# The second feed-forward product of a hybrid RWKV-7 / gMLP step, with seven block products in place of eight

## The chip, the cores and the metric

One core of one Trainium2 chip. The metric is the device time of one execution in microseconds (us); the time before is the median of three runs.

## The reference

One denoising step of a two-layer backbone. Two streams are taken together: 128 context tokens and 512 latent tokens, T = 640 columns of 1024 features. Each layer has an RWKV-7 branch and a chunked gMLP branch, a mix of both, and then the feed-forward part that the change touches:

```python
h2 = rmsnorm(x, p['norm2_g'][l]) * (1 + sc2) + sh2
x = x + g2 * (jnp.square(jax.nn.relu(h2 @ p['w1'][l])) @ p['w2'][l])
```

`w1` is 1024 x 4096, `w2` is 4096 x 1024, all in float32. Six modulation vectors (shift, scale and gate, twice) come from `silu(cond) @ w_ada + b_ada` for each layer and each of the two streams; `g2` is one of them. After the last layer follows one more RMSNorm with `final_g`.

## The kernel before, in words

Features lie on the 128 partitions, the 640 tokens along the free axis as two halves of HT = 320. A matrix of weights comes as blocks of 128x512 (four 128x128 weights side by side). `load_w` (L97 to L104) loads such a block, copies it on ACT to `hi` (the reduced type that TensorE takes, fp32r) and subtracts on DVE to get `lo`, the rest. Every product is three matmuls: `hi` by high part, `hi` by low part, `lo` by high part of the activations (`mm_block`, L106 to L113). `hi` and `lo` have four buffers each, the raw block three. `dense` (L115) makes one output block of 128 x 640 in a PSUM tile `dps` with a bank for each half; there are two such tiles, and four single banks in another pool (`psr`, tags `g` and `pu`). `dense_pair` (L262 on) makes two output blocks half by half, the first half of both before the second, so that what follows for the first half can start early; its weights are loaded and split once for each half.

The feed-forward part (mark `ff`) works in two halves of the hidden dimension. In each, 16 output blocks of the first product go through relu and square on ACT and are split into `fh` and `fl`; then the second product adds into `x`, with the hidden blocks as its inner dimension, block by block of the eight output blocks (`residual`, L271 to L276: one operation on DVE for each token range with its own gate, so 128, 192 and 320 columns). In the second half the last two output blocks go by `dense_pair`, and after each half of the tokens `after` adds to the sum of squares (`sumsq`) and starts the norm: that of layer 1 (`rms.norm`), or the final one (`fin`, L1018, with a store for each of the eight blocks).

In layer 0's first half the modulation of layer 1 is made as well. `mod_col` (L163) loads 128 columns of `w_ada` as 128x1024 and reduces it on DVE twice (once for each stream) against `silu(cond)`; 48 such columns, three after each hidden block.

All is unrolled. The framework orders each engine's instructions when the program is built: an instruction that stands earlier in the program goes first where its inputs and buffers are ready by its plan, and it sets all waits. On the chip each engine then takes its instructions in that fixed order. Loads go through SP's queue.

Of the kernel before, what the change touches and what calls it, by code (L numbers as in the profile page):

```python
# [33 lines left out]
GORD = (((0, 4), (4, 4), (8, 2)), ((0, 4), (8, 2), (4, 4)))  # L34
SP = {'n': (3, 2, 1, 2, 2, 1, 0, 0, 3, 1), 'v': 1, 'k': 4, 'r': 7, 'kk': 7, 'F': 200, 'B': None, 't': 10, 'g0': 2, 'gn': (2, 2, 2, 1, 2, 2, 2, 1)}
# [6 lines left out]
def emit(tc, I, O, depth=DEPTH, mark=lambda s: None):  # L42
    nc = tc.nc
    ctx = ExitStack()
    with ctx:
# [117 lines left out]
        def mod_col(l, j, scr):  # L163
# [95 lines left out]
        def wsrc(w):  # L259
            return lambda kb: w[:, kb * 512:(kb + 1) * 512]  # L260
# [46 lines left out]
        for l in range(depth):  # L307
# [73 lines left out]
            with tc.tile_pool(name=f"com{l}", bufs=1) as com:  # L381
# [543 lines left out]
                with tc.tile_pool(name=f"x{l}", bufs=1) as xpool:  # L925
# [38 lines left out]
                    with tc.tile_pool(name=f"ff{l}", bufs=1) as ff:  # L964
                        if l + 1 < depth:
                            mod_setup(l + 1)
                            silu_c(ff)
                        for half in range(2):
                            fh = ff.tile([128, 16, T], F32R, tag="fh", name="fh")
                            fl_ = ff.tile([128, 16, T], F32R, tag="fl", name="fl")  # L970
                            for m in range(16):
                                if half == 0 and m < 2:
                                    if m == 0:
                                        pss = dense_pair(wsrc(I["w1"][l, 0]), wsrc(I["w1"][l, 1]), hh, hl)
                                    ps = pss[m]
                                else:
                                    ps = dense(I["w1"][l, half * 16 + m], hh, hl)
                                t = ff.tile([128, T], F32, tag="nt", name="relu", bufs=3)
                                nc.scalar.activation(pv(t), ps[:, :, 0:HT], AF.Relu)
                                nc.scalar.activation(t, t, AF.Square)  # L980
                                split(fh[:, m], fl_[:, m], t)
                                if l + 1 < depth and half == 0:
# [95 lines left out]
```

## Time and profile before

| | |
|---|---|
| median of 3 runs | 3319.86 us (3317.98 to 3334.59) |
| the profiled execution | 3320.89 us, its span 3319.2 us |
| PE busy | 3129.1 us (94%), 26160 matmuls |
| DVE, ACT, POOL busy | 2156.9 (65%), 1509.4 (45%), 613.5 us (18%) |
| layer 0's feed-forward part | some 1222 to 1692 us |
| layer 1's feed-forward part | some 2847 to 3305 us |
| DMA queue q1 | 368.49 MB, 34.7% of 16 engines |

PE is the TensorE's matmuls, DVE VectorE, ACT ScalarE, POOL GpSimd. Of a matmul's busy time a good part overlaps the next one's, so the pace of matmuls is read from counts in a stretch and not from the length of one. "L111" is the line in the kernel. A group's name reads output<-inputs by the program's tile names. What stands after "<-" in brackets is what ended an idle time.

### The profile page before, as it was taken

Reading aid. Unit: us, or ns where it says so; the run is one execution under the profiler, and the core shown is the slowest. Engines: PE = TensorE matmul, PEld = TensorE weight load, DVE = VectorE, ACT = ScalarE, POOL = GpSimd, SP = SyncE. Lnnn points to the kernel's source line nnn. Section 1 sums busy time; section 2 is a strip of 40 time slices with the busy share of each in tenths; the row PEclk is TensorE's granted clock in tenths of the full one; section 3 lists DMA queues with packets and bytes.
Section 4 is the critical chain, followed back from the end, with each engine's and each line's share of the span. In section 5 each row is a group of like instructions: output and inputs, shape, how many; then the busy total and the mean of one; then the engine's idle time right before and its main releaser. Section 6 shows DMA issues by size and latency. Waiting matters only on the chain.

```text
span 3319.2 us, 66348 instructions
## 1 busy us (share of the span) xinstructions
PE 3129.1 (94%) x26160; PEld 2840.5 (86%) x26160; DVE 2156.9 (65%) x4147; ACT 1509.4 (45%) x3268; POOL 613.5 (18%) x616
## 2 busy tenths in 40 slices
PE   8999799999999999999999979999999999999998
PEld 7988677777778989999999967787777799899998
DVE  6777778878875468943363387788897735532334
ACT  5444444554555345224264434455554533541432
POOL 3004333333331010000010143333333200100000
PEclk7998889999999999999999989899999999999999
DMA  6683122222224626632344521122222345222223
GB/s 206 203 299 124 57 74 67 76 67 74 67 80 125 216 83 212 217 115 77 93 146 145 189 79 57 58 81 72 78 75 73 104 142 169 89 77 74 77 74 102
DMA packets 215671, 372.73 MB, mean 112 GB/s; under 512 B 63680, under 2 KB 72000, under 8 KB 215360
## 3 DMA queue, kind: packets, MB, share of 16 engines
q1 hardware_dynamic: 215360, 368.49, 34.7%
q8 instruction: 206, 3.38, 0.4%
q14 instruction: 105, 0.86, 0.1%
HBM read 288.41 MB, written 63.31 MB: 106 GB/s over the span
## 4 chain that ended last, share of the span: by engine, by line
PE 66%; DVE 18%; issue 5%; DMA 4%; ACT 4%; POOL 2%; SPq 0%; DVEq 0%; POOLq 0%; ACTq 0%
PE dps L111 43%; PE g L644 4%; DMA wada<-in_wada 3%; PE dps L491 3%; PE dps L256 3%; DVE D L676 2%; DVE X L678 2%; DVE wjunk L168 2%; PE pu L776 2%; PE pu L789 2%; PE pu L751 1%; PE pu L757 1%; PE pu L795 1%; DVE lo L103 1%; DVE XN L694 1%
## 5 line engine op out<-in xcount | busy, mean ns | idle before, releaser
L101 ACT ACTIVATE hi<-raw 128x512 fp32r<-128x512 f32 x630 | 396.2, 631 | 1006.6 <-PE dps L111 803.0
L103 DVE TENSOR_TENSOR lo<-raw,hi 128x512 fp32r<-128x512 f32 x550 | 393.9, 718 | 522.5 <-ACT hi L101 510.8
L111 PE MATMUL dps<-ah,hi 128*128 128x320 f32 x2768 | 685.2, 324 | 7.6 <-ACT up L468 4.1
L111 PE MATMUL dps<-ah,lo 128*128 128x320 f32 x2768 | 677.7, 321 | 0.0
L111 PE MATMUL dps<-al,hi 128*128 128x320 f32 x2768 | 677.6, 322 | 0.0
L111 PEld LDWEIGHTS dps<-ah,hi 128*128 128x128 f32 x2768 | 474.5, 192 | 26.7 <-ACT up L468 5.2
L111 PEld LDWEIGHTS dps<-ah,lo 128*128 128x128 f32 x2768 | 474.2, 192 | 14.5 <-issue 0.4
L111 PEld LDWEIGHTS dps<-al,hi 128*128 128x128 f32 x2768 | 475.0, 192 | 13.2 <-issue 0.4
L168 DVE CUSTOM_DVE_ANT_0 wjunk<-wada,sc 128x1024 f32<-128x1024 f32 x176 | 221.9, 1261 | 34.2 <-DMA wada<-in_wada 32.2
L785 POOL TENSOR_TENSOR sw<-SV,wc 64x128 f32<-64x128 f32 x288 | 150.6, 523 | 450.5 <-DVE SV L803 438.6
L644 PE MATMUL g<-LA,BK 64*128 64x128 f32 x1280 | 183.1, 315 | 34.2 <-POOL BK L625 13.4
L103 POOL TENSOR_TENSOR lo<-raw,hi 128x512 fp32r<-128x512 f32 x80 | 118.2, 1477 | 511.8 <-ACT hi L101 425.5
L111 PE MATMUL dps<-fh,lo 128*128 128x320 f32 x896 | 204.6, 310 | 3.4 <-DVE lo L103 3.4
L644 PEld LDWEIGHTS g<-LA,BK 64*128 64x128 f32 x1280 | 153.4, 211 | 62.2 <-issue 23.6
L111 PE MATMUL dps<-fh,hi 128*128 128x320 f32 x896 | 204.3, 309 | 0.0
L111 PE MATMUL dps<-fl,hi 128*128 128x320 f32 x896 | 204.1, 309 | 0.0
L676 DVE TENSOR_TENSOR D<-AA,X 128x30 f32<-128x30 f32 (+14 forms) x480 | 182.6, 380 | 24.3 <-POOL X L671 14.2
L678 DVE TENSOR_TENSOR X<-X,D 128x30 f32<-128x30 f32 (+14 forms) x480 | 176.3, 367 | 10.5
L249 POOL TENSOR_TENSOR al<-nt,ah 128x320 fp32r<-128x320 f32 x24 | 26.7, 1114 | 705.1 <-ACT ah L248 704.0
L625 POOL TENSOR_TENSOR BK<-ta,cum 64x640 f32<-64x640 f32 x64 | 128.3, 2004 | 139.2 <-DVE ta L616 108.3
L111 PEld LDWEIGHTS dps<-fh,lo 128*128 128x128 f32 x896 | 149.6, 188 | 4.7 <-DVE lo L103 4.7
L111 PEld LDWEIGHTS dps<-fl,hi 128*128 128x128 f32 x896 | 149.9, 188 | 0.0
(293 smaller groups left out, 5773.8 us busy)
## 6 DMA issues: line engine op xcount, KB each, us to landing
raw<-in_w SPq DMA_DIRECT2D x280, 256.0 KB, 2.6
raw<-in_win SPq DMA_DIRECT2D x234, 256.0 KB, 2.8
wada<-in_wada SPq DMA_DIRECT2D x88, 512.0 KB, 4.1
ld<-up SPq DMA_DIRECT2D x80, 320.0 KB, 3.5
th<-ld SPq DMA_DIRECT2D x32, 320.0 KB, 3.0
ta<-ld SPq DMA_DIRECT2D x32, 320.0 KB, 3.1
gd<-spill SPq DMA_DIRECT2D x32, 320.0 KB, 2.3
raw<-in_wo SPq DMA_DIRECT2D x40, 256.0 KB, 2.6
```

Source lines behind the costliest of these rows:

```text
L101: nc.scalar.activation(hi, raw, AF.Copy)
L103: (eng or nc.vector).tensor_tensor(lo, raw, hi.bitcast(F32), ALU.subtract)
L111: nc.tensor.matmul(ps[:, n, 0:HT], w[:, k * 128:(k + 1) * 128], xk[:, n * HT:(n + 1) * HT], start=(first and k == 0 and j == 0), stop=(las ...
L168: nc.vector.tensor_tensor_reduce(junk, wt, sc_cur[0][:, v, :], 1.0, 0.0, ALU.mult, ALU.add, mods[l][:, j, v:v + 1])
L256: nc.tensor.matmul(ps[:, n, 0:HT], w[:, k * 128:(k + 1) * 128], x[:, 4 * kb + k, hs(n)], start=(kb == 0 and k == 0 and j == 0), stop=(kb = ...
L491: nc.tensor.matmul(o, x[:, k, tk * 128:(tk + 1) * 128], w[:, kk * 256:(kk + 1) * 256], start=(k == 0 and j == 0 and tk % 2 == 0), stop=(k ...
L625: nc.gpsimd.tensor_tensor(b[s, c, 1 - h, :], rt[s], e[s], ALU.mult)
L644: nc.tensor.matmul(gs[h][:, c - c0, :], b[s, c, :, :].rearrange("p x t -> p (x t)"), la[s, c, h:h + 2, :].rearrange("p x t -> p (x t)"), s ...
L676: nc.vector.tensor_tensor(t3, AA[:, s + 1:32, s:s + 1].to_broadcast([128, n, s]), X[:, s:s + 1, 0:s].to_broadcast([128, n, s]), ALU.mult)
L678: nc.vector.tensor_tensor(X[:, s + 1:32, 0:s], X[:, s + 1:32, 0:s], t3, ALU.add)
L776: nc.tensor.matmul(pu[64 * h:64 * h + 64, d, 0, :], LA[d][:, cs[d], 2 * h, :], SV[:, us[d], h, :], start=(d == 0), stop=True, skip_group_c ...
L785: nc.gpsimd.tensor_tensor(sw[s], SV[s, both, h, :], wcu[s, both].unsqueeze(2).to_broadcast([64, 2, L]), ALU.mult)
```

## The change

The second product works in quarters of the hidden dimension (1024, that is eight hidden blocks) and in pairs of output blocks. For a pair and a quarter the weights are four blocks A11, A12 (first output block, inner blocks 0 to 3 and 4 to 7) and A21, A22 (second), 512 deep and 128 wide; the hidden activations are four blocks B11, B12 (inner blocks 0 to 3, first and second half of the tokens) and B21, B22. Eight products of such blocks become seven (Strassen's scheme in Winograd's form), each of four 128-deep steps with three matmuls of 128x320:

- `hidden` makes relu and square of eight hidden blocks, then T1 to T4 by subtraction (on POOL, for the last j on DVE), and splits all seven activation blocks into `FH`, `FL`. In layer 0 both `lo` of each `w1` block are made on POOL, in layer 1 one of the two.
- `combine` loads the four weight blocks and makes S1 to S4 by four operations on POOL, one pair ahead of use.
- `strassen` splits A11, A12, A22 and S1 to S4 (some on POOL), accumulates in four PSUM tiles a, b, c, d, copies a on ACT and adds on DVE (`u2`, `u3`, `s1`), and adds the four results into `x`. In the first pair of a quarter (`lead`) the first three products go first in their three leading steps.
- Layer 1's modulation is made by `mod_halves` in 96 steps with 512-wide reductions, four after each hidden block with j < 3 and two after each pair, in quarters 0 to 2; the remaining sums are added at its end.
- After the last pair's first half `done` starts the norm of the first half, as before; the final norm's multiplications and stores for both halves come after the second.

The diff, cut (the lines taken out are those of the kernel above; indentation shortened):

```diff
--- before
+++ after
+WB, HB = 4, 1
...
+        def mod_halves(l, scr):
+            macc = scr.tile([128, 48, 2], F32, tag="macc", name="macc")
+            for hf in range(2):
+                w = slice(512 * hf, 512 * hf + 512)
+                sc = scr.tile([128, 2, 512], F32, tag="sch", name="sch")
+                for v in range(2):
+                    nc.sync.dma_start(sc[:, v, :], I["cc"][v:v + 1, w].to_broadcast([128, 512]))
+                    th = scr.tile([128, 512], F32, tag="wjh", name="silu")
+                    nc.scalar.activation(th, sc[:, v, :], AF.Tanh, scale=0.5)
+                    nc.vector.scalar_tensor_tensor(th, th, 1.0, sc[:, v, :], ALU.add, ALU.mult)
+                    nc.vector.tensor_scalar(sc[:, v, :], th, 0.5, None, ALU.mult)
+                for j in range(48):
+                    wt = scr.tile([128, 512], F32, tag="wah", name="wah", bufs=3)
+                    nc.sync.dma_start(wt, I["wada"][l, j, :, w])
+                    junk = scr.tile([128, 512], F32, tag="wjh", name="wjh")
+                    for v in range(2):
+                        acc = macc[:, j, v:v + 1] if hf else mods[l][:, j, v:v + 1]
+                        nc.vector.tensor_tensor_reduce(junk, wt, sc[:, v, :], 1.0, 0.0, ALU.mult, ALU.add, acc)
+                    yield
+            nc.vector.tensor_tensor(mods[l], mods[l], macc, ALU.add)
...
-with tc.tile_pool(name=f"ff{l}", bufs=1) as ff:
+with tc.tile_pool(name=f"ff{l}", bufs=1) as ff, ExitStack() as ctx_l:
     if l + 1 < depth:
         mod_setup(l + 1)
-        silu_c(ff)
...
+    B11, B21, B22, T1, T2, T3, T4, B12 = range(8)
+    def w1src(m):
+        return wsrc(I["w1"][l, m])
+    def w2raw(m, q, kb):
+        return I["w2"][l, m, q, :, kb * 512:(kb + 1) * 512]
+    def hidden(q):
+        FH = ff.tile([128, 7, 4, HT], F32R, tag="fh", name="fh")
+        FL = ff.tile([128, 7, 4, HT], F32R, tag="fl", name="fl")
+        for j in range(4):
+            H = ff.tile([128, 8, HT], F32, tag="H", name="H", bufs=HB)
+            ms = (8 * q + j, 8 * q + j + 4)
+            if q == 0 and j == 0:
+                pss = dense_pair(w1src(ms[0]), w1src(ms[1]), hh, hl)
+            for z, m in enumerate(ms):
+                ps = pss[z] if q == 0 and j == 0 else dense(I["w1"][l, m], hh, hl, engs=(nc.gpsimd if l + 1 < depth else None, nc.gpsimd))
+                o = H[:, B11:B12 + 1:7, :] if z == 0 else H[:, B21:B22 + 1, :]
+                nc.scalar.activation(o, ps[:, :, 0:HT], AF.Relu)
+                nc.scalar.activation(o, o, AF.Square)
+                mod_some(4 if j < 3 else 0)
+            split(FH[:, 0:3, j, :], FL[:, 0:3, j, :], H[:, 0:3, :])
+            e = nc.vector if j == 3 else nc.gpsimd
+            e.tensor_tensor(H[:, T1], H[:, B12], H[:, B11], ALU.subtract)
+            e.tensor_tensor(H[:, T3], H[:, B22], H[:, B12], ALU.subtract)
+            e.tensor_tensor(H[:, T2], H[:, B22], H[:, T1], ALU.subtract)
+            e.tensor_tensor(H[:, T4], H[:, B21], H[:, T2], ALU.subtract)
+            split(FH[:, 3:7, j, :], FL[:, 3:7, j, :], H[:, 3:7, :])
+        return FH, FL
+    def combine(q, m0, m1):
+        A = {}
+        for z, m in enumerate((m0, m1)):
+            for kb in range(2):
+                t = A[z, kb] = ff.tile([128, 512], F32, tag="ar", name="ar", bufs=6)
+                nc.sync.dma_start(t, w2raw(m, q, kb))
+        S = [ff.tile([128, 512], F32, tag="sr", name="sr", bufs=4) for _ in range(3)]
+        nc.gpsimd.tensor_tensor(S[0], A[1, 0], A[1, 1], ALU.add)
+        nc.gpsimd.tensor_tensor(S[1], S[0], A[0, 0], ALU.subtract)
+        nc.gpsimd.tensor_tensor(A[1, 0], A[0, 0], A[1, 0], ALU.subtract)
+        nc.gpsimd.tensor_tensor(S[2], A[0, 1], S[1], ALU.subtract)
+        S.insert(2, A[1, 0])
+        return A[0, 0], A[0, 1], A[1, 1], S
+    def strassen(m0, m1, W, FH, FL, half, lead):
+        A11, A12, A22, (S1, S2, S3, S4) = W
+        a = psr.tile([128, 512], F32, tag="g", name="sa")[:, 0:HT]
+        b = psr.tile([128, 512], F32, tag="pu", name="sb")[:, 0:HT]
+        cd = dense_ps()
+        c, d = cd[:, 0, 0:HT], cd[:, 1, 0:HT]
+        def parts(w, eng=None):
+            hi = wpool.tile([128, 512], F32R, tag="hi", name="hi", bufs=WB)
+            lo = wpool.tile([128, 512], F32R, tag="lo", name="lo", bufs=WB)
+            split(hi, lo, w, eng)
+            return hi, lo
+        def mul(o, w, x, first, eng=None, ks=range(4)):
+            hi, lo = w if isinstance(w, tuple) else parts(w, eng)
+            for k in ks:
+                ks = slice(k * 128, (k + 1) * 128)
+                for jj, (w_, x_) in enumerate(((hi, FH), (hi, FL), (lo, FH))):
+                    nc.tensor.matmul(o, w_[:, ks], x_[:, x, k, :], start=(first and k == 0 and jj == 0),
+                                     stop=(k == 3 and jj == 2), skip_group_check=True)
+        def new(name):
+            return ff.tile([128, HT], F32, tag="cmb", name=name, bufs=4)
+        def add(t, p, r):
+            nc.vector.tensor_tensor(t, p, r, ALU.add)
+            return t
+        def into(src, k, n):
+            for v, lo, hi in vpieces(n):
+                nc.vector.scalar_tensor_tensor(x[:, k, lo:hi], src[:, lo - n * HT:hi - n * HT], mods[l][:, 40 + k, v:v + 1],
+                                               x[:, k, lo:hi], ALU.mult, ALU.add)
+        s1 = new("s1")
+        if lead:
+            jobs = [(o, parts(w, e), y) for o, w, y, e in ((a, A11, B11, None), (b, S2, T2, nc.gpsimd), (c, S1, T1, None))]
+            for ks in (range(3), range(3, 4)):
+                for o, w, y in jobs:
+                    mul(o, w, y, True, ks=ks)
+        else:
+            mul(a, A11, B11, True)
+        nc.scalar.activation(s1, a, AF.Copy)
+        if not lead:
+            mul(b, S2, T2, True)
+        u2 = add(new("u2"), b, s1)
+        mul(a, A12, B21, False, None if lead else nc.gpsimd)
+        into(a, m0, 0)
+        mul(b, S3, T3, False)
+        u3 = add(new("u3"), b, s1)
+        mul(d, A22, T4, True)
+        into(add(s1, d, u3), m1, 0)
+        half(0)
+        if not lead:
+            mul(c, S1, T1, True, nc.gpsimd)
+        into(add(u3, c, u3), m1, 1)
+        mul(c, S4, B22, False)
+        into(add(u2, c, u2), m0, 1)
+        half(1)
+    def quarter(q, half):
+        W = combine(q, 0, 1)
+        FH, FL = hidden(q)
+        for mp in range(4):
+            cur = W
+            if mp < 3:
+                W = combine(q, 2 * mp + 2, 2 * mp + 3)
+            strassen(2 * mp, 2 * mp + 1, cur, FH, FL, lambda n: half(mp, n), mp == 0)
+            mod_some(2)
+    mod_next = iter(())
+    def mod_some(n):
+        for _ in range(n):
+            next(mod_next, None)
+    with tc.tile_pool(name=f"ffm{l}", bufs=1) as fm:
+        if l + 1 < depth:
+            mod_next = mod_halves(l + 1, fm)
+        for q in range(3):
+            quarter(q, lambda mp, n: None)
+        if l + 1 < depth:
+            for _ in mod_next:
+                pass
             mod_early(l + 1)
             mod_late(l + 1)
...
+    ffe = ctx_l.enter_context(tc.tile_pool(name=f"ffe{l}", bufs=1))
+    rms = Rms(ffe)
     last = l == depth - 1
     if not last:
...
+        acts_next = []
+    def done(mp, n):
+        for k in (2 * mp, 2 * mp + 1):
+            sumsq(x, k, acc, ffe, (n,))
+            if not last:
+                nc.sync.dma_start(xd[l + 1][:, k, hs(n)], x[:, k, hs(n)])
+        if mp < 3:
+            return
         if not last:
...
+            if not acts_next:
+                acts_next.extend(new_acts())
+            rms.norm(x, acc, l + 1, 0, n, *acts_next)
+        else:
             rs = rms.rstd(acc, n)
...
+            for q, n in [(q, n) for n in ((), (0, 1))[n] for q in range(NK)]:
+                t = ffe.tile([128, T], F32, tag="nt", name="fin", bufs=3)
                 nc.vector.scalar_tensor_tensor(t[:, hs(n)], x[:, q, hs(n)], ftile[:, q:q + 1], rs[:, hs(n)], ALU.mult, ALU.mult)
                 nc.sync.dma_start(O["y"][:, q, hs(n)], t[:, hs(n)])
...
+    quarter(3, done)
+    if not last:
+        hh, hl = acts_next
```

## Rows read from the trace of the kernel before

**Rows 1.** stretches of both feed-forward parts: length, then busy us and instructions by engine
```profile
1262.00:1420.00 158.00, 155.02 (x1052) 153.97 (x1051) 145.85 (x250) 54.03 (x82) 0.00 (x0) 1.00 0.69 217
1460.00:1540.00 80.00, 80.00 (x548) 80.00 (x546) 25.23 (x36) 35.22 (x53) 0.00 (x0) 1.00 0.24 75
...
2900.00:3000.00 100.00, 100.00 (x684) 100.00 (x683) 30.43 (x45) 38.41 (x59) 0.00 (x0) 1.00 0.24 74
```

**Rows 2.** chain of waits in order of time, layer 1's part: start, us, what
```profile
2867.86 408.43 PE dps L111 x2784
3276.30 16.13 PE dps L256 x110
...
3292.98 12.04 PE dps L256 x82
```

**Rows 3.** TensorE's own waits from 1262 to 1655: us, times, longest
```profile
PE dps L111 <- DVE lo L103: 3.4, 5, 1.5
```

**Rows 4.** groups from 1240 to 1720: busy us, mean ns, then idle before
```profile
L168 DVE CUSTOM_DVE_ANT_0 wjunk<-wada,sc 128x1024 f32<-128x1024 f32 x96 | 117.3, 1221 | 13.7 <-DMA wada<-in_wada 12.5
...
L103 DVE TENSOR_TENSOR lo<-raw,hi 128x512 fp32r<-128x512 f32 x144 | 98.9, 689 | 125.8 <-ACT hi L101 125.8
L101 ACT ACTIVATE hi<-raw 128x512 fp32r<-128x512 f32 x144 | 90.5, 631 | 270.3 <-PE dps L111 179.0 <-DMA raw<-in_w 74.9 <-PE dps L256 9.0
...
L128 DVE TENSOR_TENSOR fl<-relu,fh 128x640 fp32r<-128x640 f32 x32 | 26.3, 823 | 24.9 <-ACT fh L127 24.9
...
L980 ACT ACTIVATE relu<-relu 128x640 f32<-128x640 f32 x32 | 23.6, 738 | 1.0
...
L979 ACT ACTIVATE relu<-dps 128x640 f32<-128x640 f32 x32 | 22.0, 688 | 3.7 <-PE dps L111 3.7
```

**Rows 5.** single POOL operations by line or tile: ns as min/median/max
```profile
L103 POOL TENSOR_TENSOR lo<-raw,hi x80: 1265/1312/2865, 237.0 to 2605.2; 128x512 fp32r<-128x512 f32 x80
...
L357 POOL TENSOR_TENSOR nt<-x,nrs x8: 1536/2500/2604, 28.5 to 58.7; 128x640 f32<-128x640 f32 x8
...
L249 POOL TENSOR_TENSOR al<-nt,ah x24: 862/986/1615, 1222.4 to 2864.9; 128x320 fp32r<-128x320 f32 x24
```

**Rows 6.** POOL in order of time in the prologue: start, us, operation
```profile
31.02 2.26 POOL L128 TENSOR_TENSOR z<-zr,z 128x512 fp32r<-128x512 f32 x1
33.23 3.03 POOL L357 TENSOR_TENSOR nt<-x,nrs 128x640 f32<-128x640 f32 x2
...
43.62 2.60 POOL L357 TENSOR_TENSOR nt<-x,nrs 128x640 f32<-128x640 f32 x1 [0.76 <-DVE al L128]
```

**Rows 7.** DVE in order of time in the same stretch
```profile
36.87 2.30 DVE L168 CUSTOM_DVE_ANT_0 wjunk<-wada,sc 128x1024 f32<-128x1024 f32 x1
...
40.52 1.21 DVE L168 CUSTOM_DVE_ANT_0 wjunk<-wada,sc 128x1024 f32<-128x1024 f32 x1
...
41.66 1.88 DVE L128 TENSOR_TENSOR al<-nt,ah 128x640 fp32r<-128x640 f32 x1
```

**Rows 8.** all engines in order of time at 1684, POOL beside DVE
```profile
1684.01 0.88 POOL L249 TENSOR_TENSOR al<-nt,ah 128x320 fp32r<-128x320 f32 x1 [438.11 <-ACT ah L248]
...
1684.01 0.54 DVE L276 SCALAR_TENSOR_TENSOR x<-dps,mod,x 128x320 f32<-128x320 f32 x1
```

**Rows 9.** DVE at the end of the kernel
```profile
3305.05 0.55 DVE L276 SCALAR_TENSOR_TENSOR x<-dps,mod,x 128x320 f32<-128x320 f32 x1 [1.44 <-PE dps L256]
...
3310.22 1.48 DVE L1018 SCALAR_TENSOR_TENSOR fin<-x,fing,nrs 128x320 f32<-128x320 f32 x3
3312.69 1.52 DVE L1018 SCALAR_TENSOR_TENSOR fin<-x,fing,nrs 128x320 f32<-128x320 f32 x3 [1.00 <-DMA out_y<-fin]
```

**Rows 10.** DVE around the change of layers, first half's norm
```profile
1676.64 0.49 DVE L203 TENSOR_TENSOR nacc<-nacc,nsq 128x320 f32<-128x320 f32 x1
...
1681.16 0.68 DVE L240 SCALAR_TENSOR_TENSOR nt<-x,mod,nrs 128x128 f32<-128x128 f32 x2
...
1690.29 0.41 DVE L243 SCALAR_TENSOR_TENSOR al<-nt,mod,ah 128x192 fp32r<-128x192 f32 x1
```

More of the change, by code (lines that the diff above doesn't have):

```diff
@@ L963, in emit @@
                     mark("ff")
-                    with tc.tile_pool(name=f"ff{l}", bufs=1) as ff:
+                    with tc.tile_pool(name=f"ff{l}", bufs=1) as ff, ExitStack() as ctx_l:
                         if l + 1 < depth:
                             mod_setup(l + 1)
-                            silu_c(ff)
[L968 to L982, printed above, removed]
-                                    for j in range(3 * m, 3 * m + 3):
-                                        mod_col(l + 1, j, ff)
-                            if l + 1 < depth and half == 0:
@@ L986, in emit @@
                                 mod_early(l + 1)
                                 mod_late(l + 1)
-                            def w2src(m):
-                                return lambda kb: I["w2"][l, m, half * 2 + kb // 2, :, (kb % 2) * 512:(kb % 2) * 512 + 512]
-                            for m in range(NK - 2 * half):
-                                ps = dense_ps()
-                                for kb in range(4):
-                                    wh, wl = load_w(w2src(m)(kb))
-                                    mm_block(ps, wh, wl, fh, fl_, kb * 4, kb == 0, kb == 3)
-                                residual(ps, x, l, 40, m)
-                                if half == 1:
-                                    sumsq(x, m, acc, ff)
-                                    if l + 1 < depth:
-                                        nc.sync.dma_start(xd[l + 1][:, m], x[:, m])
@@ L1001, in emit @@
-                        rms = Rms(ff)
+                        ffe = ctx_l.enter_context(tc.tile_pool(name=f"ffe{l}", bufs=1))
+                        rms = Rms(ffe)
                         last = l == depth - 1
                         if not last:
-                            hh, hl = new_acts()
-                        def after(ps, j, n):
-                            k = NK - 2 + j
-                            residual(ps, x, l, 40, k, (n,))
-                            sumsq(x, k, acc, ff, (n,))
+                            acts_next = []
@@ L1012, in after @@
-                            if j == 1 and not last:
-                                rms.norm(x, acc, l + 1, 0, n, hh, hl)
-                            elif j == 1:
+                                if not acts_next:
+                                    acts_next.extend(new_acts())
+                                rms.norm(x, acc, l + 1, 0, n, *acts_next)
+                            else:
                                 rs = rms.rstd(acc, n)
-                                for q in range(NK):
-                                    t = ff.tile([128, T], F32, tag="nt", name="fin", bufs=3)
+                                for q, n in [(q, n) for n in ((), (0, 1))[n] for q in range(NK)]:
+                                    t = ffe.tile([128, T], F32, tag="nt", name="fin", bufs=3)
@@ L1018, in after @@
                                     nc.vector.scalar_tensor_tensor(t[:, hs(n)], x[:, q, hs(n)], ftile[:, q:q + 1], rs[:, hs(n)], ALU.mult, ALU.mult)
                                     nc.sync.dma_start(O["y"][:, q, hs(n)], t[:, hs(n)])
-                        dense_pair(w2src(NK - 2), w2src(NK - 1), fh, fl_, 4, after)
+                        quarter(3, done)
+                        if not last:
+                            hh, hl = acts_next
 def prep(inp):
```

5 lines of the change are left out of this document (2 added, 3 removed).

## The prediction

> **What bounds the kernel now.** I read the stretches of the two feed-forward parts first, then the chain of waits, then TensorE's own waits, and only then single durations. In the stretches [rows 1] PE is busy all the time, at granted clock 1.00: 684 matmuls in 100 us, so 0.146 us from one 128x320 matmul to the next, although a single one lasts 0.31 us (they overlap). Layer 1 shows this without DVE pressure (30 of 100 us). In layer 0 DVE is busy for 146 of 158 us, because the 96 `wjunk` reductions for layer 1's modulation lie there, and PE still loses only 3 us. The chain of waits says the same: one piece of 2784 matmuls on PE in 408 us, then the last pair's matmuls [rows 2]. TensorE's own waits in layer 0's part come to 3.4 us, all for a `lo` from DVE [rows 3]. So both parts are bound by the number of matmuls: 1536 for each product, 3072 a layer, 449 us. The reader is to note one thing in rows 1: POOL does nothing in either part (0.00, x0).
>
> **The change, part by part.** *Removed.* A pair of output blocks over a quarter was 8 block products of 12 matmuls and becomes 7: 84 for 96. There are 16 such groups a layer: 192 matmuls a layer, 384 in all, 384 x 0.146 = 56 us. The new matmuls have the same shape, each still with its own weights, so I keep the 0.146. With the 3.4 us of rows 3 the gain is at most 59 us. A quarter is now 8 x 48 + 4 x 84 = 720 matmuls, 105.3 us, where before it was 112.3 us.
>
> *Added on DVE and POOL.* A pair and quarter needs seven weight splits where there were four, four subtractions or additions of weights on POOL, five additions that read PSUM, six scaled additions into `x`. The hidden part needs seven blocks split where there were four, and four subtractions to make them; in layer 0 POOL also makes both `lo` of every first-product weight. Single durations: DVE 0.69 for 128x512, 0.82 for 128x640, 1.22 for the 1024-wide reduction [rows 4]; back to back each starts 0.07 to 0.08 before the one ahead ends (the reduction at 40.52 and the `al` at 41.66 [rows 7]), so 0.61, 0.74 and 1.15 of pace, and by the straight line through these 0.41 for 320, 1.07 for 960, 1.40 for 1280 and 0.61 for a 512-wide reduction. POOL: 1.27 for 128x512 and 0.88 for 128x320, when alone [rows 5, 8].
>
> Taken engine by engine all this fits under PE. It does not, because the two engines take turns. In the prologue, the one place where both have work all the time, a POOL operation that takes 1.27 or 1.54 alone [rows 5] takes 1.9 to 2.6 [rows 6], and DVE's reduction of 1.21 takes 2.30 beside it [rows 7]: each waits for the other to finish. From 31.02 to 46.19, 15.2 us, POOL did three of 1.27 and four of 1.54, 10.0 us, and DVE did four reductions (one of them begun a little before), two 640-wide `al` and seven tiny operations, 6.9 us at its pace. The sum is 16.9, so the turns overlap by 1.7 us over 7 POOL operations, 0.24 us each. A DVE operation with one operand in PSUM does not take a turn: an `x` update of 128x320 keeps 0.54 while POOL runs its 0.88 from the same instant [rows 8].
>
> Now one quarter of layer 0 with reductions (quarters 0 to 2, each with 32 of the 96 half-columns, 64 reductions of 512). Hidden part: DVE 4 x (1.07 + 1.40) for the block splits, 4 x 0.41 for the last four subtractions, 48 x 0.61 for reductions, 40.8 us; POOL 16 x 1.27 for `lo`, 12 x 0.88 for the other subtractions, 4 x 1.27 to combine the first pair's weights, 36.0 us. Less 32 overlaps of 0.24: 69 us, against PE's 56.1. The four pairs: DVE 21 splits x 0.61, twelve updates of `x` from SBUF (1.5 us a pair: 0.59 for the two pieces of the first half, 0.46 for each of the others), 16 x 0.61, 28.6 us; POOL 7 splits and 12 combinations x 1.27, 24.1 us. Less 19 x 0.24: 48 us against PE's 49.1. So the hidden part is bound by the turns at 69 us or more, and the pairs are bound by both at once. No queue is ever perfectly filled: DVE's and POOL's instructions are in a fixed order with waits for PE and ACT between them. I add 5% to the hidden part (73) and 4 us to the pairs (53): 126 us a quarter, between 112 (turns hide better, PE nearly the bound) and 140 (they lose 15%). Quarter 3 has no reductions: 117 less 39 is 78 us of turns, PE bound, 105.3.
>
> The Trainium skill's page "SBUF — State Buffer", section "SBUF: two separate sides", says that VectorE (with two SBUF inputs) and GpSimd share a pair of ports as an exclusive lock for the whole instruction. Rows 6 and 7 agree with a lock, but show 0.24 us of overlap per operation. By the page's whole instruction a quarter is 129.5 us of turns instead of 117, and the sum would be some 37 us longer.
>
> *Start of a quarter's products.* They need the last hidden block. After its last matmul come relu 0.69 and square 0.74 on ACT, three subtractions of 0.49 on DVE (the 1.0 us ACT copy of the first three blocks beside them), the 1280-wide copy, about 1.3 by rows 4, and its `lo`, 1.48: 5.7 us, with small gaps 6.2. Three quarters of the first three products, 27 matmuls, 3.95 us, and three more lie ready. That leaves 1.7 us, and 1.2 more if the first `lo` is ahead on DVE. I take 2.5 a quarter (0 to 6). Before, the last hidden block was first needed some 90 matmuls into the second product, so nothing waited. *Inside the pairs* four weight buffers now cover four times 12 matmuls, half as long as before, and c's second product waits until DVE has read the first; the next pair's first product can stand in. I take 2 us a quarter (0 to 5). Layer 0's quarter 3 and layer 1's four quarters then take 110 us each.
>
> *Ends.* In layer 1 all 16 last multiplications (`fin`) now come after the second half; three of them take 2.47 us, held by their stores [rows 9], so 8 more cost 6.6, and one more addition 0.5, the first half's root 0.4: 7.5 (6 to 10). Between the layers the first half's norm ran from 1681 to 1691 under the second half's 96 matmuls (14 us); now 24 matmuls (3.5 us) are left to cover it, while next-layer products can start as its blocks come [rows 10]. Of 10.5 us of lost cover I take 8 (2 to 14).
>
> *Sum.* Layer 0: 3 x 126 + 110 = 488 against 449 + 3, +36. Layer 1: 4 x 110 = 440 against 449, -9. Ends +15.5. In all +42 on the profiled execution of 3320.89 us (span 3319.2), which lies 1.0 us above the median of 3319.86: 3362 for the median.
>
> **Rivals.** *PE stays the bound in layer 0.* For it: before, DVE at 92% cost PE only 3 us, since the reductions wait for nobody and the order can slip them into gaps. Against: then POOL was idle [rows 1]. Layer 0 would be 4 x 110 = 440, and the whole -12 - 9 + 15.5 = -6, 3314; with no stalls in the quarters (-36) 3278. It wins from a mean quarter of 110.6 us down: 452 and 449 are eight of 112.6, and the ends take 15.5 / 8. *Turns at their best.* The hidden part loses nothing over 69 us and the pairs run at 50: 119 a quarter, 108 where there are no reductions: layer 0 +13, layer 1 -17, ends +9: +5, 3325. *Splits late in every pair.* With buffers for 7 us of matmuls and POOL queued behind four chained combinations, each `lo` made by POOL comes late in layer 1 too: a middle pair there holds 12.2 us of turns (4.6 on DVE, 7.6 on POOL) against 12.3 of PE. At 1.5 us in each of 32 pairs that is 48 less the 16 already taken, +74 in all: 3394. *Fewer matmuls than said* is excluded by the code: 84 a pair.
>
> **How the numbers follow.** What a measurement here can tell from no change is about 0.5%, 16.6 us. The forecast has 0.50 (0.03 of it within the 0.5%), late splits 0.14, turns at their best 0.16 (0.04 faster, 0.09 the same, 0.03 slower), PE the bound 0.20 (0.12 faster, 0.08 the same). That is faster 0.16, same 0.20, slower 0.64. The forecast's own spread, 3 x (112 to 140) with the ends at 8 to 24, is 3313 to 3412. With a tenth left out on either side the range is 3295 to 3420.
>
> **What would show it.** Right: in quarters 0 to 2 of layer 0's part 0.17 us or so per matmul, POOL's 128x512 above 1.8 us and DVE's two-operand ones above their 0.69 there; layer 1's part at 0.15; 16 `fin` at the end. Wrong: 0.146 throughout layer 0 with POOL near 1.27 (the turns don't bind), or layer 1 stalling as much as layer 0 (then it is the splits' lateness). The whole forecast falls if layer 0's part gets shorter than 449 us.

## The result, and the profile after

The changed kernel takes 3432.24 us (median of 6 runs, 3410.88 to 3439.24) against 3329.81 us for the kernel before (6 runs, 3317.98 to 3354.22). The ratio is 1.0305, 95% interval 1.0273 to 1.0336. The sign was forecast; the size was not: 3362 was predicted, 3295 to 3420 as the range.

The two profiled executions reach layer 0's part (first matmul of the last `wo` pair) at 1205.6 us before and 1190.0 after, though nothing differs ahead of it but 41 reductions. I therefore compare lengths of stretches, cut at the same matmul. "Loss" below is a stretch's length less its matmuls in the program times 0.1465 us (rows count one or two more, those that overlap the edge). The cuts count the norm's few small matmuls too, so that each "last product" lies some 0.8 us early, in every kernel alike; differences don't feel it.

| stretch | before | after | difference |
|---|---|---|---|
| layer 0's part, `wo` pair to last product | 485.5 | 561.2 | +75.7 |
| change of layers and layer 1's branches | 1143.3 (mean of 7 profiles with layer 0 as before) | 1153.4 (mean of 9 with it changed) | +10 |
| layer 1's part | 478.2 | 481.9 | +3.7 |
| after the last product matmul (the tail) | 15.4 | 22.7 | +7.3 |

The sum is +97, near the 102 between the medians. First, layer 0 of the changed kernel, which answers to the first two lines of [rows 1]; the stretches are the start (both pairs by halves) and the four quarters; columns as there.

```profile
1189.99:1239.36 49.37, 36.10 (x194) 31.53 (x193) 48.14 (x108) 27.86 (x57) 11.70 (x10) 0.90 0.44 136
1239.36:1379.63 140.27, 107.68 (x626) 103.11 (x625) 119.73 (x207) 47.23 (x71) 76.61 (x51) 0.87 0.42 130
1379.63:1518.41 138.78, 116.23 (x721) 112.58 (x721) 120.85 (x219) 47.88 (x73) 74.24 (x51) 0.92 0.38 119
1518.41:1634.04 115.63, 108.68 (x722) 105.61 (x721) 59.78 (x78) 49.52 (x74) 70.68 (x51) 1.00 0.24 74
1634.04:1751.14 117.10, 109.36 (x722) 105.70 (x721) 67.80 (x95) 54.67 (x89) 62.78 (x45) 1.00 0.26 81
```

The last busy times before the clock are DVE, ACT and POOL. In quarter 0 DVE (120) and POOL (77) together show 196 us of busy time in 140, and PE is idle for a quarter of it, a sixth in quarter 1. The losses are 21.2, 48.9, 33.3, 10.2 and 11.6, 125 us in all, against 21 before. 192 matmuls less give back 28, hence +75.7. Within a quarter the hidden part of quarters 2 and 3 takes 56.4 us for 384 matmuls: full pace. The whole loss there is in the pairs. Where the 192 `wjh` reductions stand (DVE alone; one that crosses an edge counts on both sides):

```profile
1100.00:1189.99 89.99, 27.73 (x41) 1.00 0.73 235
1189.99:1239.36 49.37, 16.90 (x21) 0.90 0.44 136
1239.36:1291.45 52.09, 35.85 (x33) 0.97 0.53 164
1291.45:1379.63 88.18, 33.68 (x33) 0.82 0.35 110
1379.63:1447.90 68.27, 57.40 (x55) 0.94 0.50 160
1447.90:1518.41 70.51, 8.27 (x12) 0.90 0.27 80
1518.41:1634.04 115.63, 0.00 (x0) 1.00 0.24 74
```

The fixed order put a third of them ahead of quarter 0, the rest into quarters 0 and 1, none into quarter 2. PE's own waits from 1240 to 1520, where [rows 3] had 3.4 us (us, times, longest):

```profile
PE dps L112 <- ACT H L1008: 13.1, 4, 5.4
PE sa L1052 <- DVE lo L129: 12.3, 5, 3.6
PE dps L112 <- POOL lo L104: 7.1, 3, 3.1
PE sa L1052 <- ACT fh L128: 5.0, 1, 5.0
```

The first is the single buffer `H`: relu of the next hidden block waits until DVE has split the last one, and that split stands behind reductions. In order of time (start, us) at the first pair of quarter 0:

```profile
1279.25 1.01 ACT L128 ACTIVATE fh<-H 128x960 fp32r<-128x960 f32 x1
1285.19 1.27 ACT L128 ACTIVATE fh<-H 128x1280 fp32r<-128x1280 f32 x1 [4.93 <-POOL H L1016]
...
1291.02 0.69 DVE L188 CUSTOM_DVE_ANT_0 wjh<-wah,sch 128x512 f32<-128x512 f32 x1 [0.66 <-DMA wah<-in_wada]
...
1291.64 1.16 DVE L129 TENSOR_TENSOR fl<-H,fh 128x960 fp32r<-128x960 f32 x1
...
1293.32 1.49 DVE L129 TENSOR_TENSOR fl<-H,fh 128x1280 fp32r<-128x1280 f32 x1
1294.72 0.68 DVE L129 TENSOR_TENSOR lo<-ar,hi 128x512 fp32r<-128x512 f32 x1
1294.90 0.70 ACT L1008 ACTIVATE H<-dps 128x640 f32<-128x640 f32 x1 [7.39 <-DVE fl L129]
...
1295.46 0.42 PE L1052 MATMUL sa<-fh,lo 128*128 128x320 f32 x1 [3.55 <-DVE lo L129]
...
1297.06 0.47 PE L1052 MATMUL sb<-fh,hi 128*128 128x320 f32 x1
1297.33 0.47 PE L1052 MATMUL sb<-fl,hi 128*128 128x320 f32 x1
```

The first `fl` could have started when its `fh` was there, at 1280.26; DVE ran reductions until 1291.64. The second `fh` was itself 4.93 us late, for POOL's T4. ACT lost 7.39 us and PE 3.55. From 1296.0 to 1299.4, right after that wait, the granted clock is 0.50, and PE starts a matmul every 0.27 us in place of 0.146.

Layer 1, one hidden part and the pairs after it, against the last line of [rows 1]: the hidden part runs at full pace with POOL busy for 24 us, the pairs lose 7.1.

```profile
3045.88:3102.19 56.31, 56.31 (x386) 56.31 (x385) 21.86 (x19) 26.04 (x37) 24.04 (x20) 1.00 0.25 76
3102.19:3158.60 56.41, 52.41 (x338) 49.32 (x337) 46.22 (x67) 22.20 (x36) 35.36 (x23) 1.00 0.24 75
```

These pairs (2985 to 3390) by kind of operation on DVE: busy us, mean ns, idle before. Operations with both operands in SBUF are longer than without POOL (`lo` took 689 ns in [rows 4]; `x<-u` takes 545 in e7 below). Those that read PSUM (`sb`, `dps`, `sa`) are not: 483 and 346 ns in e7 for the last two here.

```profile
L129 DVE TENSOR_TENSOR lo<-ar,hi 128x512 fp32r<-128x512 f32 x52 | 53.1, 1021 | 12.0 <-ACT hi L128 11.3
L129 DVE TENSOR_TENSOR lo<-sr,hi 128x512 fp32r<-128x512 f32 x32 | 36.8, 1150 | 3.4 <-ACT hi L128 2.9
L1064 DVE SCALAR_TENSOR_TENSOR x<-u,mod,x 128x320 f32<-128x320 f32 x32 | 27.4, 857 | 0.6
...
L1059 DVE TENSOR_TENSOR u<-sb,s 128x320 f32<-128x320 f32 x32 | 15.4, 482 | 2.1 <-PE sb L1052 1.7
...
L1064 DVE SCALAR_TENSOR_TENSOR x<-sa,mod,x 128x128 f32<-128x128 f32 x16 | 5.5, 345 | 7.4 <-PE sa L1052 7.4
```

The end, as in [rows 9]: 16 `fin` behind the last product in place of 8, three in 2.5 us, held by their stores.

```profile
3394.89 1.48 DVE L1140 SCALAR_TENSOR_TENSOR fin<-x,fing,nrs 128x320 f32<-128x320 f32 x3
3397.38 1.50 DVE L1140 SCALAR_TENSOR_TENSOR fin<-x,fing,nrs 128x320 f32<-128x320 f32 x3 [1.01 <-DMA out_y<-fin]
...
3404.78 1.07 DVE L1140 SCALAR_TENSOR_TENSOR fin<-x,fing,nrs 128x320 f32<-128x320 f32 x2 [0.93 <-DMA out_y<-fin]
```

### The profile page after: what moved, and what is told of

Same layout as the page of the kernel before. It is cut to its first block, busy times and chain, and to the rows that moved or that the text cites. A ratio compares the mean times of both kernels' runs of the same rounds, so it can differ in the third digit from the quotient of the medians.

```text
span 3409.2 us, 66805 instructions
## 1 busy us (share of the span) xinstructions
PE 3114.4 (91%) x25776; PEld 2798.8 (82%) x25776; DVE 2446.1 (72%) x4576; ACT 1589.8 (47%) x3394; POOL 1141.5 (33%) x986
## 3 DMA queue, kind: packets, MB, share of 16 engines
q1 hardware_dynamic: 221120, 364.30, 33.3%
## 4 chain that ended last, share of the span: by engine, by line
PE 38%; DVE 10%; ACT 3%; issue 3%; POOL 2%; DMA 0%; SPq 0%; DVEq 0%; ACTq 0%; POOLq 0%
PE dps L112 22%; PE dps L1052 3%; PE g L666 2%; PE dps L513 2%; PE sb L1052 2%; PE sa L1052 1%; DVE X L700 1%; DVE lo L129 1%; DVE D L698 1%; PE pu L798 1%; DVE x L1064 1%; PE pu L811 1%; PE pu L773 1%; PE pu L779 1%; PE pu L817 1%
## 5 line engine op out<-in xcount | busy, mean ns | idle before, releaser
L102 ACT ACTIVATE hi<-raw 128x512 fp32r<-128x512 f32 x486 | 303.0, 629 | 607.8 <-PE dps L112 418.8
L104 POOL TENSOR_TENSOR lo<-raw,hi 128x512 fp32r<-128x512 f32 x170 | 251.9, 1485 | 639.3 <-ACT hi L102 550.1
L104 DVE TENSOR_TENSOR lo<-raw,hi 128x512 fp32r<-128x512 f32 x316 | 244.5, 777 | 208.1 <-ACT hi L102 194.9
L129 DVE TENSOR_TENSOR fl<-H,fh 128x960 fp32r<-128x960 f32 x64 | 101.3, 1583 | 166.7 <-ACT fh L128 165.4
L188 DVE CUSTOM_DVE_ANT_0 wjh<-wah,sch 128x512 f32<-128x512 f32 x192 | 179.8, 937 | 8.5 <-DMA wah<-in_wada 4.5
L647 POOL TENSOR_TENSOR BK<-ta,cum 64x640 f32<-64x640 f32 x64 | 130.3, 2035 | 138.1 <-DVE ta L638 112.7
L128 ACT ACTIVATE hi<-ar 128x512 fp32r<-128x512 f32 x128 | 80.3, 629 | 169.4 <-PE dps L1052 80.3
L1052 PE MATMUL dps<-fh,hi 128*128 128x320 f32 x384 | 125.8, 328 | 17.7 <-DVE u L1059 12.4
L677 DVE TENSOR_TENSOR GR<-g,m_inc 128x128 f32<-128x128 f32 (+1 forms) x192 | 72.6, 378 | 82.9 <-ACT TT L676 79.3
L1052 PE MATMUL dps<-fh,lo 128*128 128x320 f32 x384 | 122.6, 319 | 3.8 <-DVE lo L129 3.0
L1052 PE MATMUL dps<-fl,hi 128*128 128x320 f32 x384 | 121.4, 316 | 0.0
```

Of the source, the lines that this page charges most:

```text
L104: (eng or nc.vector).tensor_tensor(lo, raw, hi.bitcast(F32), ALU.subtract)
L128: nc.scalar.activation(hi, x, AF.Copy)
L129: (eng or nc.vector).tensor_tensor(lo, x, hi.bitcast(F32), ALU.subtract)
L188: nc.vector.tensor_tensor_reduce(junk, wt, sc[:, v, :], 1.0, 0.0, ALU.mult, ALU.add, acc)
L647: nc.gpsimd.tensor_tensor(b[s, c, 1 - h, :], rt[s], e[s], ALU.mult)
L1052: nc.tensor.matmul(o, w_[:, ks], x_[:, x, k, :], start=(first and k == 0 and jj == 0), stop=(k == 3 and jj == 2), skip_group_check=True)
```

## The experiments

The theory: POOL and DVE's operations on two SBUF operands take turns, and the reductions, ahead of the splits in DVE's fixed order, carry that to TensorE. Rivals: DVE has too much to do whatever POOL does; the weights that POOL makes are simply late; ACT's wait for the second half of the condition in the middle of the part.

**e1, e3 and a control: short reductions.** Edit (e3 also leaves POOL's work out of both layers; e8 makes the same cut in the kernel before):

```diff
-  nc.vector.tensor_tensor_reduce(junk, wt, sc[:, v, :], 1.0, ...
+  nc.vector.tensor_tensor_reduce(junk[:, 0:16], wt[:, 0:16], sc[:, v, 0:16], 1.0, ...
```

> Layer 0's 192 reductions for layer 1's modulation are cut from 512 to 16 columns (so the modulation is not computed, all instructions and loads stay). Theory A (the reductions take turns with POOL and stand in VectorE's fixed order ahead of the splits that TensorE waits for): quarters 0 and 1 fall from 143 and 137 us to the 116 of quarter 2, the start of the part by 8: some 55 to 60 us less than the changed kernel. Rival B (the stalls are the splits' own: one buffer H, POOL's long chain, four weight buffers): under 20 us less, quarters 0 and 1 stay above 130. Rival C (the middle wait of ACT for the second condition half): it stays, 18 us of the 70 stay.

> POOL's work is left out of the feed-forward part in both layers, and the reductions are 16 columns wide. Theory A: layer 0's four quarters run at 106 to 109 us. For layer 1's 7.2 us a quarter: if they are the quarter's start (last hidden block to first product) and the u additions of the first pair, 5 to 7 stay, 111; if they are POOL's late parts, 1 to 2 stay, 107. In all 85 to 95 us less than the changed kernel in the first case, 105 to 115 in the second.

> The kernel before, its 96 reductions cut from 1024 to 16 columns (the modulation is then not computed). A control for the short reductions: before, they were hidden, so the time should be the same within 0.2% (3 us in layer 0's part). If reductions cost more than their waits show (by the clock, or by memory traffic), it is 10 us or more faster. The length of layer 1's RWKV stretch in its profile (1134.5 before, 1153.4 after) also tells whether that difference is chance.

Measured: e1 1.0223 (1.0185 to 1.0261), 28 us less, half of what the theory wanted. e3 1.0020 (0.9995 to 1.0045), 93 us less. e8 1.0008 (0.9994 to 1.0022): hidden before, as said, though layer 0's part is 6 us longer in its profile. But e1 is not clean: short reductions outrun their loads, and DVE, in order, waits for these ahead of the splits (1150 to 1560):

```profile
DVE wjh L188 <- DMA wah<-in_wada: 47.3, 53, 4.8
```

In e3 that is 57.2 us, and its first pairs lose 16.7. What e3 does settle is layer 1, where there are no reductions: its pairs lose 2.2 us a quarter in place of 7.1 (3.8 in place of 10.3 in the last), so the greater part comes with POOL's work. DVE does as many operations there (66 and 67 in a quarter's pairs), but nothing waits for POOL's results any more. e8's stretch between the layers took 1141.0 us: the 1134.5 of the profile before lay low by chance.

**e2: no POOL in layer 0's part.** The low parts that POOL made become `hi`, T and S plain blocks:

```diff
+  if l + 1 < depth:
+      return A[0, 0], A[0, 1], A[1, 1], [A[1, 0], A[0, 0], A[0, 1], A[1, 1]]
   S = [ff.tile([128, 512], F32, tag="sr", ...
```

> In layer 0's feed-forward part everything POOL did is left out (the low parts it made are replaced by the high ones, T1 to T4 and S1 to S4 by plain blocks; the last j of a quarter keeps its subtractions on VectorE); the reductions stay whole. Theory A in its narrow form (turns between POOL and VectorE's two-operand instructions): reductions back at 0.69 us, quarters 0 and 1 at 106 to 112, quarters 2 and 3 at 108: 75 to 85 us less than the changed kernel. Rival D (VectorE's fixed order alone: reductions ahead of the splits, whatever POOL does): quarters 0 and 1 stay above 125, at most 40 us less.

Measured 1.0057 (1.0033 to 1.0080), 82 us less; layer 0's part 483.1 in place of 561.2, with all the reductions and these in the same places (22, 65, 67 and none in the start and quarters 0 to 2). DVE's order alone (rival D) falls. The reductions of quarters 0 and 1, first in the changed kernel, then here:

```profile
L188 DVE CUSTOM_DVE_ANT_0 wjh<-wah,sch 128x512 f32<-128x512 f32 x131 | 135.1, 1031 | 7.6 <-DMA wah<-in_wada 4.5
L191 DVE CUSTOM_DVE_ANT_0 wjh<-wah,sch 128x512 f32<-128x512 f32 x131 | 90.3, 689 | 13.0 <-DMA wah<-in_wada 10.0
```

Quarters 0 and 1 still lose 9.7 and 11.1 us, more than was expected, quarters 2 and 3 2.4 and 4.2: so some 7 us a quarter come with the reductions even when POOL is idle. And the run also leaves out what was late.

**e6: POOL's work moved to DVE, nothing left out** (the sums as here, T1 to T4 and the low parts likewise).

```diff
-  nc.gpsimd.tensor_tensor(S[0], A[1, 0], A[1, 1], ALU.add)
+  nc.vector.tensor_tensor(S[0], A[1, 0], A[1, 1], ALU.add)
...
```

> As the changed kernel, with all that POOL does in the feed-forward parts (combinations, T1 to T4, its low parts) moved to VectorE, both layers; nothing is left out. Turns theory: although VectorE gets 39 us a quarter more in layer 0's hidden part and pairs, layer 0's part gets shorter, from 561 to some 500 us, and layer 1's pairs lose 2 to 4 us a quarter in place of 7.1: some 70 us less than the changed kernel. Rival (what counts is the amount of work on VectorE, and its fixed order): layer 0's part stays at 561 or grows, layer 1 loses 7 or more a quarter.

Measured 1.0018 (1.0003 to 1.0033), 3333.64 us, 98.6 less than the changed kernel (96 by the two ratios), where 70 were expected. The same five stretches of layer 0, now 481.6:

```profile
1215.64:1262.62 46.98, 35.73 (x194) 32.06 (x193) 46.15 (x108) 27.93 (x58) 8.78 (x8) 0.85 0.43 138
1262.62:1360.32 97.70, 93.90 (x626) 91.58 (x625) 94.25 (x202) 48.06 (x72) 0.00 (x0) 1.00 0.47 147
1360.32:1474.36 114.04, 109.77 (x722) 108.28 (x721) 109.13 (x246) 48.69 (x73) 0.00 (x0) 0.97 0.47 141
1474.36:1584.07 109.71, 108.01 (x722) 105.63 (x721) 96.57 (x211) 49.34 (x73) 0.00 (x0) 1.00 0.38 119
1584.07:1697.20 113.13, 108.70 (x722) 105.68 (x721) 77.46 (x140) 55.46 (x89) 0.00 (x0) 1.00 0.27 83
```

DVE now does everything, is busy for 109 of 114 us in quarter 1, and still quarter 0 is 43 us shorter. So the amount of work was not too much. The order is not held fixed here: 37, 58 and 38 reductions now stand in quarters 0 to 2, in place of 65, 67 and none. What part of the gain comes from that e6 can't tell; e2, which keeps the places, and e9 and e10 below, which add nothing but POOL's work, show that the second engine does the harm.

**e13: no reductions, no loads for them** (`mods` is set to a constant; POOL stays).

> As the changed kernel without the 192 reductions and without their loads and silu (layer 1's modulation is then not computed); POOL's work stays. If reductions and POOL together make the loss (turns, with the reductions ahead of splits): quarters 0 and 1 lose what quarter 2 lost, 10 to 12 us in the pairs and nothing in the hidden part; layer 0's part falls from 561 to 490 to 500, the whole by 60 to 70. If the reductions' share is the 30 us that the short ones gave back: 531 and 30.

Measured 1.0114 (1.0068 to 1.0159), 69 us less by the medians and 64 by the two ratios; layer 0's part 495.5, quarter by quarter (the first three lines: start, quarters 0 and 1):

```profile
1219.78:1262.06 42.28, 35.88 (x194) 33.28 (x193) 33.40 (x67) 28.95 (x58) 10.98 (x10) 0.84 0.28 87
1262.06:1365.30 103.24, 96.36 (x626) 93.00 (x625) 58.19 (x75) 45.23 (x69) 71.36 (x53) 0.98 0.29 90
1365.30:1482.19 116.89, 110.14 (x721) 107.18 (x721) 60.41 (x77) 47.92 (x72) 70.50 (x51) 0.98 0.24 73
```

All four quarters lose 10 to 12 us, all in the pairs. So neither alone makes the loss: reductions without POOL (e6) leave 46 us of it in this part, POOL without reductions 60, both 125; before it was 21.

**e14: POOL out of the hidden part alone** (T1 to T4 and low parts of `w1` on DVE).

> As the changed kernel, but what POOL does for the hidden blocks (T1 to T4, low parts of the first product's weights) goes to VectorE in both layers; combinations and low parts for the pairs stay on POOL. Turns theory: in the hidden part VectorE has 41 + 16 x 0.61 + 12 x 0.41 = 55 us against TensorE's 56, so h0 and h1 lose under 5 in place of 9 to 12; the pairs still take turns with POOL and with what reductions fall there: layer 1's pairs keep their 7, layer 0's p0 and p1 lose 15 to 25 in place of 39 and 22. Layer 0's part 515 to 530. Rival (the whole amount on both engines counts, wherever): no shorter than 550.

Measured 1.0236 (1.0195 to 1.0277); layer 0's part 527.8. The hidden parts of quarters 0 and 1 lose 0.7 and 0.1, as expected; their pairs 26.4 and 25.6, a little over what was expected (39.5 and 21.7 in the changed kernel); those of layer 1 7.1. Place matters: what is left on POOL costs where it stands.

**e9: POOL additions that nobody waits for, in the kernel before.**

```diff
   split(fh[:, m], fl_[:, m], t)
+  for z in range(3):
+      nc.gpsimd.tensor_tensor(idle, fh[:, m, 0:512].bitcast(F32), fh[:, m, 128:640].bitcast(F32), ALU.add)
```

> The kernel before, plus three POOL additions of 128x512 after each hidden block's split (48 a half, 192 in all), whose result nobody reads and nobody waits for. Turns theory: each takes VectorE's two-operand work away for 1.0 us. Layer 0's first half, where VectorE was busy 92% of the time, gets 15 to 40 us longer; layer 0's second half and layer 1, where VectorE has room, lose 0 to 3 us each; the reductions take above 1.6 us beside POOL in place of 1.2. Rival (POOL costs only where something waits for POOL's results): within 3 us of the kernel before everywhere.

Measured 1.0137 (1.0095 to 1.0179), 45 us more, just over the range expected. Layer 0's first half takes 259.3 us in place of 216.0; its second half 227.6 in both, layer 1 478.2 in both. So 48 additions cost 43 us where DVE was full, and the other 144 nothing. DVE's groups there (1240 to 1400) and a stretch of layer 1 that answers to the last of [rows 1], with 20 us of POOL in it:

```profile
L168 DVE CUSTOM_DVE_ANT_0 wjunk<-wada,sc 128x1024 f32<-128x1024 f32 x56 | 93.0, 1661 | 2.1 <-DMA wada<-in_wada 1.4
L103 DVE TENSOR_TENSOR lo<-raw,hi 128x512 fp32r<-128x512 f32 x33 | 37.3, 1129 | 2.0 <-ACT hi L101 2.0
```

```profile
3000.00:3100.00 100.00, 100.00 (x684) 100.00 (x683) 29.99 (x48) 26.62 (x41) 20.45 (x13) 1.00 0.25 77
```

The rival (late results) predicted nothing at all here, and falls as the sole cause. That it has a share in layer 0 of the changed kernel stays possible: PE's own waits for POOL's `lo` were 7.1 us there.

**e4, e7, e10: layer 0 as before.** e4 has layer 1 as changed; e7 puts its POOL work on DVE and the first half's `fin` early again; e10 adds to e7:

```diff
   FH, FL = hidden(q)
+  for z in range(24):
+      nc.gpsimd.tensor_tensor(idle, FH[:, 3:5, 3, 0:256].bitcast(F32), FH[:, 5:7, 3, 0:256].bitcast(F32), ALU.add)
```

> Layer 0's feed-forward part as before, layer 1's as changed. By the offsets of the two traces layer 1's part costs +4 us and the tail +7: +11 us over the kernel before (0.3%), if the drift of 8 us in layer 1's RWKV stage came with layer 0's change or by chance; +20 if it comes back here. If layer 1's loss were caused by something left over from layer 0 it would be -10.

> Layer 0 as before; layer 1 as changed, but with POOL's work on VectorE and the first half's last multiplications early. Turns theory: layer 1's part 478 to about 463 us, tail as before: 15 us under the kernel before (ratio 0.995). Rival (late weights whatever engine makes them): layer 1's part 480, ratio 1.000 or above.

> As the kernel with layer 0 as before and layer 1's seven products all on VectorE, plus 24 POOL additions of 128x512 in each of layer 1's quarters, ready when the hidden part ends; nobody reads them. In the four pairs VectorE has about 43 us of work by its single durations against TensorE's 49. Turns theory: 43 + 24 x 1.03 = 68 us, so the pairs lose 10 to 20 us a quarter in place of 4.1. Rival (lateness of what POOL makes): the pairs keep their 4.1.

Measured: e4 1.0038 (1.0014 to 1.0061), as expected. e7 0.9977 (0.9957 to 0.9998), 3321.92 us: the one version whose interval lies below 1, just so. It misses both things expected: its layer 1 part fell to 469.5 and not to 463, 8.7 under the kernel before, and its tail stayed at 23.5, 8.1 over. By its own stretches the gain is 0.6 us, and I do not call the rest shown. With the `fin` of the first half early in the program the last stretch is as long, since they run behind the last product all the same, now ahead of the second half's sums. The last product's last matmul, the first half's `nrs` and `fin`, then the sums and PE's wait for them:

```profile
3290.38 0.31 PE L1113 MATMUL dps<-fh,lo 128*128 128x320 f32 x1
3291.14 0.48 DVE L249 SCALAR_TENSOR_TENSOR nrs<-newton,nrs 128x320 f32<-128x320 f32 x1
...
3292.00 1.47 DVE L1201 SCALAR_TENSOR_TENSOR fin<-x,fing,nrs 128x320 f32<-128x320 f32 x3
...
3298.42 0.49 DVE L225 TENSOR_TENSOR nacc<-nacc,nsq 128x320 f32<-128x320 f32 x1 [0.40 <-ACT nsq L224]
...
3299.99 1.44 PE L237 MATMUL rps<-nacc,ones_f 128*128 128x320 f32 x2 [9.30 <-DVE nacc L225]
```

e10 1.0258 (1.0215 to 1.0302). The pairs of one quarter, e7 and then e10:

```profile
3014.62:3067.87 53.25, 51.53 (x338) 49.31 (x337) 46.01 (x89) 22.32 (x36) 0.00 (x0) 1.00 0.26 83
```

```profile
3052.61:3124.81 72.20, 58.07 (x338) 54.64 (x337) 66.96 (x89) 22.33 (x36) 38.05 (x24) 0.91 0.20 61
```

The same 89 operations keep DVE busy for 67 us in place of 46. Over the four quarters the pairs of e10 lose 24.9 us on the mean in place of 4.8, more than the 10 to 20 expected: 0.84 us for each addition that nobody reads.

**e5: silu ahead, `fin` early.** Both halves of the condition are loaded and go through silu before the first reduction.

> As the changed kernel, with two edits in separate stretches: both halves of the condition go through silu ahead of the reductions (no ACT wait for a load in the middle), and the first half's eight last multiplications go early again, as before. Theory C: the first quarter's pairs lose 14 us less than the 39.5 they lose over TensorE's pace. Rival: only the place of the stall moves, and that stretch keeps its loss within 4 us. Tail: 15.4 us after the last product in place of 22.7 if the eight late multiplications are its cause. Together some 20 us less than the changed kernel, 7 by the rival.

Measured 1.0290 (1.0255 to 1.0325), 5 us less. The first pairs lose 36.4 in place of 39.5: the rival holds, the stall only moved. The tail is 23.5: as in e7, the early `fin` still run behind the last product (from 3397.93 on), so order alone doesn't give it back.

**e11, e12: changes of order on top of e7 and e6.** In a quarter's first pair d's product goes ahead of a's second; in the last quarter both last pairs' first halves come before their second halves. Both also have one more buffer for `sr` and for the sums, and e12, like e7, has the first half's `fin` early.

> Layer 0 as before; layer 1 with all on VectorE, with two changes of order: in a quarter's first pair the product for d goes ahead of a's second one (it covers the copy of a), and in the last quarter the first halves of both last pairs come before their second halves (48 matmuls in place of 24 between the last first-half product and the end). If the quarter's 4.1 us are the start and the copy: 2.5 to 3 stay. If the tail of 23.5 us comes from the short cover: 20. Together 8 us less than without them, ratio to before 0.9955; if neither is the cause, 0.9977 as without them.

> As the one above, but both layers with seven products, all on VectorE. From the parts measured (layer 0's part 481.6 against 485.5, the change of layers some 8 to 10 us longer, less 3 us for the longer cover and 1.2 a quarter): within 3 us of the one above, ratio 0.996 to 0.998.

Measured: e11 0.9986 (0.9962 to 1.0010), e12 1.0022 (1.0000 to 1.0044). A miss: the quarters of e11 still lose 4.2 us, the last one 1.1 more than in e7, and the tail is 22.0; e12 is 13 us above e11 where at most 3 were expected. What the 4.2 are made of stays open but for the 2.3 that e3 leaves.

## Why the prediction was wrong in size

The sign came out as forecast. By stretches the sum was +42 and is +97: layer 0's part +75.7 where I had +36, layer 1's +3.7 where I had -9, the ends +17 where I had +15.5.

- *Removed: 384 matmuls at 0.146.* Right: 56.3 us for 384 in every undisturbed hidden part, 192 matmuls fewer a layer.
- *Turns of POOL and DVE.* Right in kind, and now shown by e2, e9 and e10: DVE's SBUF operations of 0.69 us take 1.02 to 1.15, PSUM ones stay. POOL's 128x512 ones came to 1.36 to 1.76 us on the mean in quarters 0 and 1, under the 1.8 that I gave as a sign. The Trainium skill's "SBUF — State Buffer", section "SBUF: two separate sides", has VectorE (with two SBUF inputs) and GpSimd hold their shared ports in turn, each for its whole instruction. Here an addition that takes 1.26 to 1.29 us at its shortest cost 0.90 (e9) and 0.84 (e10) of TensorE's time, after what slack DVE had; these runs don't decide between the whole and the 1.03 that I took.
- *The step that failed: "I add 5% to the hidden part (73) and 4 us to the pairs (53)".* The hidden part was put too high: it lost 9 and 12 us in quarters 0 and 1, where I had 17. The pairs were far too low: 39.5 and 21.7 with reductions, and 10 to 11.4 without any (quarters 2 and 3, and all four of e13), where I had 4 and, for quarter 3, 4.5. Over layer 0 that is 21 us in the hidden parts where I had 51, and 83 in the pairs where I had 16; that the two errors have opposite signs is luck. I had the sum of the turns (48) under PE's 49.1 and took that for nearly hidden. The framework put 33 reductions into quarter 0's pairs where I had 16; at my own prices that makes 58 us and a loss of 9, not 39.5. My reading of the rest, from PE's waits for DVE's `lo`, `fl` and `u`, and not tested by itself: a pair has short chains (weights to `hi` to `lo`, product to `u` to product) through the same two engines, each link waits for a turn, and at equal load such waits reach TensorE. "Splits late in every pair" stood among the rivals with 1.5 us a pair; it should have been added to the turns, not set against them: 1.8 us a pair in layer 1, 2.6 in layer 0.
- *Reductions in quarters 0 to 2.* Partly wrong: they ran ahead of quarter 0 (a third) and in quarters 0 and 1. Quarter 2 thus lost 10 and not 20, but the start lost 21 us in place of 14. e13 gives that start back (42.3 us against 41.8 before), so the reductions, their loads and silu among the norm's operations are its cause.
- *Layer 1: 110 us a quarter, -9.* Measured 112.7 and +3.7; the term mis-sized is again the pairs, 7.1 us for 4.5, and 10.3 in the last quarter. With all on DVE (e7) it is 109.7 and -8.7, but the last quarter's pairs still lose 6.9.
- *Ends: 7.5 and 8.* Measured 7.3 and 10. Size and reason of the first were right: 16 `fin` run behind the last product. But they don't come late by their place in the program: in e7, which has the first half's early, its `nrs` ends 0.9 us after the last product matmul. What is missing is cover, 24 matmuls behind the first half where there were 96; 48 (e11) gave back 1.5 us. The second is a difference between means of profiles, and what it is made of stays open.
- *PE stays the bound* and *turns at their best* are out; *fewer matmuls than said* too.

## What to carry to other kernels

Before giving work to an idle engine, ask what it shares with the busy one: here the same operations cost 98.6 us more with part of them on an idle POOL than with all on a DVE that was already busy (e6, where the reductions moved too). Where two engines' summed time comes near the bound, don't ask whether the sum fits but how long the chains through them are. Taking out an eighth of a product's matmuls pays only as far as starts, chains and ends stay covered: of 28 us in layer 1, 8.7 were left at best (e7), and the tail took 8.1 of these.

## What the runs showed beyond that

- POOL's price went with DVE's slack: 144 additions that nobody reads cost nothing where DVE was busy for a third of the time, 48 cost 43 us in a half where it had been busy for 175 of 216 us, and for 88 of the first 99 (both e9).
- A wait costs TensorE more than itself. In the changed kernel's quarters 0 and 1 the granted clock is 0.87 and 0.92 (its levels are 1.2 and 2.4 GHz, 0.50 and 1.00, so by these means a quarter and a sixth of the time at the lower), in quarters 2 and 3 1.00. After the 3.55 us wait that ended at 1295.46 the granted clock was 0.50 from 1296.0 to 1299.4, and matmuls started 0.27 us apart.
- A reduction made too short to matter can cost more than it saves: cut to 16 columns it waits for its load, in order, ahead of the splits.
